# A two-layer hybrid block on one core: three layer norms summed by GpSimd, three residual groups turned by DMA

## Chip, cores, metric

One core of one Trainium2 chip. The metric is the device time of one execution in microseconds (us). The engines are TensorE (PE; its weight load is PEld), VectorE (DVE), ScalarE (ACT), GpSimd (POOL) and SyncE (SP), which here only issues DMAs.

## The reference

A sequence of 16 meta tokens and 256 input tokens (the padding ahead of them is masked), 1024 features, goes through two layers. Each has a mixer (retention, a gated recurrence and differential attention, gated and summed) and a convolutional feed-forward, each ahead of it a norm over features and behind it a residual sum; a last norm closes it:

```python
def _rms(x):
    xf = x.astype(F32)
    return xf * lax.rsqrt(jnp.mean(xf * xf, axis=-1, keepdims=True) + EPS)
...
    for li in range(DEPTH):
...
        h = h + mixer(rms_norm(h, norm_mix_g[li]), w_in[li], w_branch[li], w_out[li], lbs[li],
                      da_lambda[li], da_subln_g[li], lambda_init, valid, pos)
        h = h + conv_ffn(rms_norm(h, norm_ffn_g[li]), w_ffn_in[li], ffn_conv_w[li], ffn_conv_b[li],
                         w_ffn_out[li], valid)
    h = rms_norm(h, norm_final_g)
    return h[:, PAD:]
```

All arithmetic is float32.

## The kernel before

The residual stream `h` stays in SBUF with features on partitions: 8 blocks of 128 features by 272 tokens. All weights pass through one stream of 128x128 tiles in the order of their use, 8 tiles (512 KB) to a chunk. For each chunk SP loads `wraw` (3 buffers), ScalarE writes its rounded upper half `whi` (4 buffers) and VectorE the rest `wlo = wraw - whi` (4 buffers). A product of the stream is three TensorE matmuls, `whi` x upper half, `whi` x lower half, `wlo` x upper half of the moving operand (lines 940 to 942). One pair of output tiles takes 16 products where there are 1024 input features; the results lie in PSUM (`main`, 2 buffers of 2 banks; for some feed-forward pairs `fi`, from the pools `bank` and `acc` of 2 banks each). Helpers record all other operations, so most rows carry line 628.

**Order.** `_trace` runs over `ORDER`, the list of output pairs of a layer (projections, `b0` to `b2`, the output projection `wo`, the feed-forward input `fi` with 22 pairs, its output `fo`), and records each operation with a due time; `_Plan.order` then lays them out by a list scheduler with costs of its own, which decides the order on each engine. Every engine works its list strictly in that order. The stream's products keep their order on TensorE; other matmuls are placed between them.

**The norms.** `Norm.square` sums the squares of the 8 blocks to two sums per token and partition; `Norm.mean` adds these two and multiplies by `ones_d`, a 128x128 matrix of 1/1024, on TensorE (tile `ms`, a PSUM bank), which sums over partitions and repeats the mean on all of them. `Norm.finish` makes `rstd` of it, by a logarithm and an exponential on ScalarE. There are four: ahead of the mixer of layer one (at the kernel's start, with its adds on GpSimd), ahead of the feed-forward of layer one, ahead of the mixer of layer two and ahead of the feed-forward of layer two. In the third the last block comes late: `mean` runs on the other seven and `finish` adds a second matmul for the eighth (`self.rest`). Meanwhile the next stage's products already run on the unscaled `h`; the first four pairs are multiplied by `rstd` when they leave PSUM (`two_a`), and from the fifth pair on the input tiles `xh`, `xl` are made again from `y = h * rstd`.

**The last groups.** `final` computes the feed-forward output of layer two with tokens on partitions: four groups, 2 token blocks by 2 halves of 512 features, each in its own PSUM bank (`fo`), 22 products of three matmuls of 512 columns each (lines 1496 to 1498). The last three products of each group come group by group, so that the groups end 2.05 us after one another. The residual is brought to this layout by 16 TensorE transposes of `h` (4 per group), which are the first to write the banks; the products add to them. Then, per group, ScalarE squares (`sq`, with a sum per token), VectorE multiplies by the gain (`y`), and with both halves of a token block done their factor (`dm`) is applied and the rows are written to `out`.

Of the kernel before, what the change touches and what calls it, by code (L numbers as in the profile page):

```python
# [15 lines left out]
U16 = mybir.dt.uint16  # L16
AF = mybir.ActivationFunctionType
# [670 lines left out]
def _trace(ctx, tc, plan, a, depth, probe):  # L688
# [32 lines left out]
    def gate_tile(name):  # L721
        return new(gp, [P, KD, T], F32, "gate", 3, name)
# [7 lines left out]
    def bank(name):  # L730
        return new(bp, [P, 512], F32, "bank", 2, name)
# [108 lines left out]
    class Norm:  # L840
# [29 lines left out]
        def mean(self):  # L870

            tt(self.acc[:, 0, :], self.acc[:, 0, :], self.acc[:, 1, :], ADD)
            self.ps = bank("ms")[:, self.first : T]
            pe.matmul(self.ps, ones_d, self.acc[:, 0, :], start=True, stop=self.rest is None)

        def finish(self):
            if self.rest is None:
                self.mean()
            else:
                pe.matmul(self.ps, ones_d, self.rest, start=False, stop=True)  # L880
            rsqrt(rstd[:, self.first :], self.ps)

        def next(self):

# [134 lines left out]
    for li in range(depth):  # L1019
# [436 lines left out]
        def values(ps, vt, e):  # L1456
# [4 lines left out]
            to_tokens(src, vt, e)  # L1461
            return src

        def final():

            turns.pop(0)
            le_set()
            hi, lo = st["ghi"], st["glo"]
            accs = [[acc_bank("fo") for _ in range(2)], [bank("fo") for _ in range(2)]]
            plan.key = clock[0] - 6.0  # L1470
            gain = gate_tile("gain").rearrange("p k t -> p (k t)")[:, :D]
            sync.dma_start(gain, a["gl"])
            y = gate_tile("y").rearrange("p k t -> p (k t)")[:, : 2 * D].rearrange("p (t d) -> p t d", t=2)
            sq = gate_tile("sq").rearrange("p k t -> p (k t)")[:, : 2 * D].rearrange("p (t d) -> p t d", t=2)
            tokens = lambda t: slice(META + t * P, META + (t + 1) * P)
            plan.key = clock[0] - 1.0
            for t in range(2):
                for k in range(KD):
                    pe.matmul(accs[t][k // 4][:, k % 4 * P : (k % 4 + 1) * P], h[:, k, tokens(t)], ident, is_transpose=True, start=k % 4 == 0, stop=False)
            cost = 3 * (BANK / 2400 + 0.0133)  # L1480
            groups = [(t, c) for t in range(2) for c in range(2)]
            chunks = {}
            order = [(k, t, c) for k in range(FK - LATE) for t, c in groups]
            order += [(k, t, c) for t, c in groups for k in range(FK - LATE, FK)]
            red = temp(12, "dm")
            for k, t, c in order:
                plan.key = clock[0]
                if k not in chunks:
                    chunks[k] = weights.chunk()
                cols = slice(c * BANK, (c + 1) * BANK)  # L1490
                wh, wl = (x[:, cols] for x in chunks[k])
                gh, gl = (x[k // 4][:, k % 4, t * P : (t + 1) * P] for x in (hi, lo))
                o = accs[t][c]

                def run(o=o, wh=wh, wl=wl, gh=gh, gl=gl, end=k == FK - 1):
                    nc.tensor.matmul(o, gh, wh, start=False, stop=False)  # L1496
                    nc.tensor.matmul(o, gl, wh, start=False, stop=False)  # L1497
                    nc.tensor.matmul(o, gh, wl, start=False, stop=end)  # L1498

                plan.main.append(plan.add("pe", run, cost, [o], [wh, wl, gh, gl]))  # L1500
                clock[0] += cost
                if k < FK - 1:
                    continue
                plan.key = clock[0]
                ms = [red[:, 4 * t + i : 4 * t + i + 1] for i in range(4)]
                act.activation(sq[:, t, cols], o, AF.Square, accum_out=ms[c])
                if c == 0:

                    ts(ms[2], ms[0], 1.0 / D, EPS, MUL, ADD)
                    tt(y[:, t, cols], o, gain[:, cols], MUL)  # L1510
                    continue
                act.activation(ms[3], ms[1], AF.Ln, scale=1.0 / D, bias=ms[2])
                act.activation(ms[3], ms[3], AF.Exp, scale=-0.5)
                stt(y[:, t, cols], o, ms[3], gain[:, cols], MUL, MUL)
                act.activation(y[:, t, :BANK], y[:, t, :BANK], AF.Copy, scale=ms[3])
                for c, queue in ((1, sync), (0, act_queue)):
                    cols = slice(c * BANK, (c + 1) * BANK)
                    queue.dma_start(a["out"][:, t * D + c * BANK : t * D + (c + 1) * BANK], y[:, t, cols])

        for name, j in ORDER:  # L1520
# [112 lines left out]
            elif name == "fi":  # L1633
                ps = products(lambda k: x_tile(k, norm.folded), name, j, t0)
                first = META if last else 0
                if j % 4 == 0:
                    for n in ("ghi", "glo"):
                        g = slot(n, F32R)[:, : 4 * (T - first)]
                        st.setdefault(n, []).append(g.rearrange("p (a t) -> p a t", a=4))
                if j < ASIDE:  # L1640
                    plan.key += LATER
                u = ps if isinstance(ps, list) else [ps[:, f, :] for f in range(2)]
# [61 lines left out]
```

## Time and profile before

| | |
|---|---|
| runs | median 1282.17 us of 3 (1281.99 to 1282.75) |
| the profiled execution | 1282.95 us, span 1281.1 us |
| instructions in the span | 28467 |
| granted TensorE clock, mean | 0.997 |

The span runs from the first to the last instruction or transfer that the profile shows; the rest of the execution's time lies around it. Rows of a timeline give start, duration, engine, line, operation, output <- inputs and, in brackets, the engine's idle time before and what ended it. Rows of a tile give the least, median and largest duration in ns. In a list of waits stand the sum of us, the number of times and the longest.

### The profile page before, as it was taken

The numbers are of one execution on the slowest core, as the hardware profiler recorded it, in microseconds if no ns is written. First come the engines' busy times: TensorE is split into PE (matmuls) and PEld (weight loads), VectorE is DVE, ScalarE is ACT, GpSimd is POOL, SyncE is SP. The second block draws the span as 40 slices with busy tenths as digits, with TensorE's granted clock in tenths as the row PEclk, the third lists the DMA queues.
The fourth block names the chain that finished last, engine by engine and source line by source line (L and its number), as shares of the span: only waits on it lengthen the run. The fifth ranks groups of instructions, "written<-read, shape, count | busy, mean of one in ns | idle before, by whom it ended". The sixth has DMA issues, their size and how long they took to land.

```text
span 1281.1 us, 28467 instructions
## 1 busy us (share of the span) xinstructions
PE 1270.9 (99%) x11630; PEld 1248.0 (97%) x11630; DVE 934.8 (73%) x1601; ACT 858.9 (67%) x1498; POOL 101.1 (8%) x82
## 2 busy tenths in 40 slices
PE   9999999999999999999999999999999999999998
PEld 9999999999999999999999999999999999999986
DVE  6787476898575789886576774757976867898843
ACT  6766677759697576665456566776587975776643
POOL 3000041101111000000000000411011110000000
PEclk9999999999999999999999999999999999999999
DMA  7554557555746545556555545575556465465653
GB/s 266 196 167 155 161 163 196 170 181 149 206 125 213 182 153 194 179 169 195 172 175 181 166 152 180 162 202 166 182 155 215 150 204 196 154 211 183 212 186 111
DMA packets 100179, 228.50 MB, mean 178 GB/s; under 512 B 46288, under 2 KB 46416, under 8 KB 100048
## 3 DMA queue, kind: packets, MB, share of 16 engines
q1 hardware_dynamic: 99760, 226.15, 55.9%
q8 instruction: 91, 1.49, 0.5%
q10 hardware_dynamic: 288, 0.52, 0.1%
q14 instruction: 40, 0.33, 0.1%
HBM read 216.16 MB, written 1.05 MB: 170 GB/s over the span
## 4 chain that ended last, share of the span: by engine, by line
PE 98%; DMA 0%; DVE 0%; issue 0%; ACT 0%; SPq 0%
PE main L940 28%; PE main L941 28%; PE main L942 28%; PE fo L1496 2%; PE fo L1497 2%; PE fo L1498 2%; PE lev L1111 1%; PE fi L940 1%; PE fi L941 1%; PE fi L942 1%; PE ds L1359 1%; PE ho L628 1%; PE ro L628 1%; PE do L628 1%; PE s L628 0%; DMA wraw<-in_w 0%
## 5 line engine op out<-in xcount | busy, mean ns | idle before, releaser
L628 DVE TENSOR_TENSOR wlo<-wraw,whi 128x1024 fp32r<-128x1024 f32 (+1 forms) x411 | 501.9, 1225 | 224.4 <-ACT whi L628 222.7
L940 PE MATMUL main<-xh,whi 128*128 128x272 f32 (+1 forms) x2240 | 644.4, 288 | 2.6 <-ACT whi L628 1.3
L942 PE MATMUL main<-xh,wlo 128*128 128x272 f32 (+1 forms) x2240 | 636.8, 284 | 0.2 <-DVE wlo L628 0.2
L941 PE MATMUL main<-xl,whi 128*128 128x272 f32 (+1 forms) x2240 | 636.8, 284 | 0.0
L628 ACT ACTIVATE whi<-wraw 128x1024 fp32r<-128x1024 f32 (+1 forms) x411 | 426.5, 1041 | 209.4 <-PE main L941 123.3
L940 PEld LDWEIGHTS main<-xh,whi 128*128 128x128 f32 x2240 | 422.4, 189 | 3.2 <-ACT whi L628 1.5
L941 PEld LDWEIGHTS main<-xl,whi 128*128 128x128 f32 x2240 | 422.4, 189 | 1.3 <-issue 1.1
L942 PEld LDWEIGHTS main<-xh,wlo 128*128 128x128 f32 x2240 | 422.4, 189 | 0.4 <-DVE wlo L628 0.4
L628 POOL PARTITION_ALL_REDUCE hr<-hsq x36 | 71.9, 2023 | 564.2 <-ACT hsq L628 393.7
L628 DVE SCALAR_TENSOR_TENSOR two_b<-main,small,two_b 128x256 f32<-128x256 f32 (+2 forms) x128 | 54.4, 485 | 28.3 <-ACT two_b L628 28.3
L628 ACT ACTIVATE two_b<-main,small 128x272 f32<-128x272 f32 (+1 forms) x64 | 33.1, 568 | 31.1 <-PE main L942 30.4
L940 PE MATMUL main<-ghi,whi 128*128 128x272 f32 x176 | 51.0, 290 | 0.0
L941 PE MATMUL main<-glo,whi 128*128 128x272 f32 x176 | 50.6, 287 | 0.0
L942 PE MATMUL main<-ghi,wlo 128*128 128x272 f32 x176 | 50.3, 286 | 0.0
L940 PE MATMUL main<-b0hi,whi 128*128 128x272 f32 (+1 forms) x128 | 37.3, 291 | 0.0
L940 PE MATMUL main<-b1hi,whi 128*128 128x272 f32 (+1 forms) x128 | 37.1, 290 | 0.0
L940 PE MATMUL fi<-xh,whi 128*128 128x272 f32 (+1 forms) x128 | 36.6, 286 | 0.0
L940 PE MATMUL main<-yhi,whi 128*128 128x272 f32 (+1 forms) x128 | 36.4, 284 | 0.0
L942 PE MATMUL main<-yhi,wlo 128*128 128x272 f32 (+1 forms) x128 | 36.3, 284 | 0.0
L941 PE MATMUL main<-b1lo,whi 128*128 128x272 f32 (+1 forms) x128 | 36.3, 284 | 0.0
L941 PE MATMUL main<-ylo,whi 128*128 128x272 f32 (+1 forms) x128 | 36.3, 284 | 0.0
L941 PE MATMUL main<-b0lo,whi 128*128 128x272 f32 (+1 forms) x128 | 36.3, 284 | 0.0
(242 smaller groups left out, 2035.1 us busy)
## 6 DMA issues: line engine op xcount, KB each, us to landing
wraw<-in_w SPq DMA_DIRECT2D x402, 512.0 KB, 3.6
turned<-apart SPq DMA_TRANSPOSE x80, 2.5
h<-in_h SPq DMA_DIRECT2D x4, 272.0 KB, 6.3
dec<-in_dec SPq DMA_DIRECT2D x2, 544.0 KB, 4.5
wraw<-in_w SPq DMA_DIRECT2D x4, 256.0 KB, 5.2
const<-in_const SPq DMA_DIRECT2D x1, 937.0 KB, 8.0
gain<-in_gl SPq DMA_DIRECT2D x1, 512.0 KB, 4.7
out<-y ACTq DMA_DIRECT2D x2, 256.0 KB, 2.8
```

The lines of the kernel that those rows point to most:

```text
L628: self.plan.add(self.name, lambda: f(*args, **kw), cost, outs, ins, kind)
L940: nc.tensor.matmul(o, wh, hi, start=first, stop=False)
L941: nc.tensor.matmul(o, wh, lo, start=False, stop=False)
L942: nc.tensor.matmul(o, wl, hi, start=False, stop=last)
L1111: nc.tensor.matmul(o, keys, x, start=True, stop=True)
L1359: nc.tensor.matmul(ss[m][:, at : at + nk], q[half, hd, q0 : q0 + P], k[half, hd, :nk], start=True, stop=True)
L1496: nc.tensor.matmul(o, gh, wh, start=False, stop=False)
L1497: nc.tensor.matmul(o, gl, wh, start=False, stop=False)
L1498: nc.tensor.matmul(o, gh, wl, start=False, stop=end)
```

## The change

Two parts. First, the three norms whose adds are on VectorE no longer use TensorE: the two sums (and for the third norm the eighth block) are added by VectorE, GpSimd sums over the partitions (`partition_all_reduce`, as it does for the head norms already), and the logarithm takes 1/1024 as its scale. The norm at the start keeps its matmul. Second, of the four last groups only the last keeps its transposes. For the other three a new function `residual`, called at the third feed-forward pair of layer two, parts `h` into upper and lower 16-bit halves (`apart`), has SP turn each by a transposing DMA (`turned`), and joins them in `old`, with due times 20 us apart; the end of each such group adds `old` to the product on VectorE before the square.

```diff
         def mean(self):
             tt(self.acc[:, 0, :], self.acc[:, 0, :], self.acc[:, 1, :], ADD)
-            self.ps = bank("ms")[:, self.first : T]
-            pe.matmul(self.ps, ones_d, self.acc[:, 0, :], start=True, stop=self.rest is None)
+            if self.adds is pool:
+                self.ps = bank("ms")[:, self.first : T]
+                pe.matmul(self.ps, ones_d, self.acc[:, 0, :], start=True, stop=True)
 
         def finish(self):
             if self.rest is None:
                 self.mean()
             else:
-                pe.matmul(self.ps, ones_d, self.rest, start=False, stop=True)
-            rsqrt(rstd[:, self.first :], self.ps)
+                tt(self.acc[:, 0, :], self.acc[:, 0, :], self.rest, ADD)
+            if self.adds is pool:
+                rsqrt(rstd[:, self.first :], self.ps)
+                return
+            total = self.acc[:, 1, :]
+            pool.partition_all_reduce(total, self.acc[:, 0, :], P, ReduceOp.add)
+            rsqrt(rstd[:, self.first :], total, 1.0 / D)
...
+        def residual():
+
+            t = gate_tile("old").rearrange("p k t -> p (k t)")
+            st["sq"] = t[:, :BANK]
+            st["old"] = t[:, BANK : 4 * BANK].rearrange("p (g d) -> p g d", g=3)
+            plan.key = clock[0] + 20.0
+            for g, (t, c) in enumerate(((0, 0), (0, 1), (1, 0))):
+                apart, turned = planes("apart", 4 * P), planes("turned", 4 * P)
...
+                for i in range(2):
+                    act.activation(apart[:, i].rearrange("p (k x) -> p k x", k=4), halves(h[:, 4 * c : 4 * c + 4, META + t * P : META + (t + 1) * P], i), AF.Copy)
+                for i in range(2):
+                    sync.dma_start(turned[:, i].rearrange("p (b x) -> p b x", x=P), apart[:, i], transpose=True)
+                for i in range(2):
+                    act.activation(halves(st["old"][:, g : g + 1], i), turned[:, i].unsqueeze(1), AF.Copy)
+                plan.key += 20.0
...
-            for t in range(2):
-                for k in range(KD):
-                    pe.matmul(accs[t][k // 4][:, k % 4 * P : (k % 4 + 1) * P], h[:, k, tokens(t)], ident, is_transpose=True, start=k % 4 == 0, stop=False)
+            for k in range(4):
+                pe.matmul(accs[1][1][:, k * P : (k + 1) * P], h[:, 4 + k, tokens], ident, is_transpose=True, start=k == 0, stop=False)
...
-                act.activation(sq[:, t, cols], o, AF.Square, accum_out=ms[c])
+                if not turned:
+                    tt(y[:, t, cols], o, old[:, 2 * t + c], ADD)
+                    o = y[:, t, cols]
+                act.activation(sq, o, AF.Square, accum_out=ms[c])
```

What it does to the order on the engines is shown at three places. On TensorE, at the start of the last groups (`fo` are the four PSUM banks, `const` holds the identity matrix, `ghi` and `glo` the feed-forward's inner activations), there stood before:

```order
L942 MATMUL main_965_2180<-xh1_14_89,wlo381_2186 128x258
L628 MATMUL fo_967_2188<-const_4_79,h_3_78 128x128
L628 MATMUL fo_968_2189<-const_4_79,h_3_78 128x128
L628 MATMUL fo_969_2190<-const_4_79,h_3_78 128x128
L628 MATMUL fo_970_2191<-const_4_79,h_3_78 128x128
```

and so on to the sixteenth transpose. Now there stand:

```order
L948 MATMUL main_969_2184<-xh1_14_89,wlo381_2190 128x258
L1520 MATMUL fo_971_2192<-whi382_2200,ghi_899_1994 128x512
L1521 MATMUL fo_971_2192<-whi382_2200,glo_900_1995 128x512
L1522 MATMUL fo_971_2192<-wlo382_2201,ghi_899_1994 128x512
L1520 MATMUL fo_972_2193<-whi382_2200,ghi_899_1994 128x512
L1521 MATMUL fo_972_2193<-whi382_2200,glo_900_1995 128x512
L1522 MATMUL fo_972_2193<-wlo382_2201,ghi_899_1994 128x512
L1520 MATMUL fo_973_2194<-whi382_2200,ghi_899_1994 128x512
L1521 MATMUL fo_973_2194<-whi382_2200,glo_900_1995 128x512
L1522 MATMUL fo_973_2194<-wlo382_2201,ghi_899_1994 128x512
L628 MATMUL fo_974_2195<-const_4_79,h_3_78 128x128 x4
L1520 MATMUL fo_974_2195<-whi382_2200,ghi_899_1994 128x512
```

Twelve transposes are gone, and the other four stand behind the first product of three groups.

On ScalarE, at the norm ahead of the feed-forward of layer two (the number behind `whi` is that of the weight chunk), there stood before:

```order
L628 ACTIVATE whi343_2016<-wraw343_2015 128x1024
L583 ACT_TABLE_LOAD
L628 ACTIVATE rstd_18_93<-ms_900_1989,eps_9_84 128x272
L628 ACTIVATE rstd_18_93<-rstd_18_93 128x272
L628 ACTIVATE whi344_2023<-wraw344_2022 128x1024
L628 ACTIVATE two_b_905_2000<-two_a_904_1999,small_1_76 128x256 x2
```

and now:

```order
L628 ACTIVATE whi343_2013<-wraw343_2012 128x1024
L583 ACT_TABLE_LOAD
L628 ACTIVATE rstd_18_93<-sum_891_1962,eps_9_84 128x272
L628 ACTIVATE whi344_2027<-wraw344_2026 128x1024
L628 ACTIVATE rstd_18_93<-rstd_18_93 128x272
L628 ACTIVATE whi345_2030<-wraw345_2029 128x1024
```

The logarithm reads GpSimd's sum (`sum`) in place of TensorE's (`ms`), and the split of chunk 344 has moved between logarithm and exponential.

On ScalarE, at the end (the four squares, the factors `dm`, the scaling of a first half `y`, the output DMAs), there stood before:

```order
L628 ACTIVATE sq_973_2194,dm_974_2195<-fo_968_2189 128x512
L628 ACTIVATE dm_974_2195<-dm_974_2195 128x1 x2
L628 ACTIVATE y_972_2193<-y_972_2193,dm_974_2195 128x512
L628 DMA out<-y_972_2193 128x512
L628 ACTIVATE sq_973_2194,dm_974_2195<-fo_969_2190 128x512
L628 ACTIVATE sq_973_2194,dm_974_2195<-fo_970_2191 128x512
```

and now:

```order
L628 ACTIVATE old_908_2015,dm_977_2198<-y_976_2197 128x512 x2
L628 ACTIVATE dm_977_2198<-dm_977_2198 128x1 x2
L628 ACTIVATE y_976_2197<-y_976_2197,dm_977_2198 128x512
L628 ACTIVATE old_908_2015,dm_977_2198<-y_976_2197 128x512
L628 DMA out<-y_976_2197 128x512
L628 ACTIVATE old_908_2015,dm_977_2198<-fo_974_2195 128x512
```

Three squares read `y`, that is, VectorE's sum, in place of PSUM, and the first output DMA on this queue has moved behind the third square.

More of the change, by code (lines that the diff above doesn't have):

```diff
@@ L1462, in values @@
             return src
+        def residual():
[5 more added lines that the diff above has]
+                apart, turned = planes("apart", 4 * P), planes("turned", 4 * P)
+                halves = lambda x, i: x.bitcast(U16).rearrange("p k (x two) -> p k x two", two=2)[:, :, :, i]
+                for i in range(2):
[5 more added lines that the diff above has]
+                plan.key += 20.0
         def final():
@@ L1473, in final @@
             y = gate_tile("y").rearrange("p k t -> p (k t)")[:, : 2 * D].rearrange("p (t d) -> p t d", t=2)
-            sq = gate_tile("sq").rearrange("p k t -> p (k t)")[:, : 2 * D].rearrange("p (t d) -> p t d", t=2)
-            tokens = lambda t: slice(META + t * P, META + (t + 1) * P)
+            sq, old = st["sq"], st["old"]
+            tokens = slice(META + P, T)
             plan.key = clock[0] - 1.0
-            for t in range(2):
-                for k in range(KD):
-                    pe.matmul(accs[t][k // 4][:, k % 4 * P : (k % 4 + 1) * P], h[:, k, tokens(t)], ident, is_transpose=True, start=k % 4 == 0, stop=False)
+            for k in range(4):
+                pe.matmul(accs[1][1][:, k * P : (k + 1) * P], h[:, 4 + k, tokens], ident, is_transpose=True, start=k == 0, stop=False)
             cost = 3 * (BANK / 2400 + 0.0133)
@@ L1493, in final, with run @@
                 o = accs[t][c]
-                def run(o=o, wh=wh, wl=wl, gh=gh, gl=gl, end=k == FK - 1):
-                    nc.tensor.matmul(o, gh, wh, start=False, stop=False)
+                turned = (t, c) == (1, 1)
+                def run(o=o, wh=wh, wl=wl, gh=gh, gl=gl, first=k == 0 and not turned, end=k == FK - 1):
+                    nc.tensor.matmul(o, gh, wh, start=first, stop=False)
                     nc.tensor.matmul(o, gl, wh, start=False, stop=False)
@@ L1639, in _trace @@
                         st.setdefault(n, []).append(g.rearrange("p (a t) -> p a t", a=4))
+                if last and j == 2:
+                    key = plan.key
+                    residual()
+                    plan.key = key
                 if j < ASIDE:
```

## Prediction

> **What bounds the kernel now.** The first view is the page: busy time by engine, then the chain that ended last, by engine.
>
> ```profile
> PE 1270.9 (99%) x11630; PEld 1248.0 (97%) x11630; DVE 934.8 (73%) x1601; ACT 858.9 (67%) x1498; POOL 101.1 (8%) x82
> ...
> PE 98%; DMA 0%; DVE 0%; issue 0%; ACT 0%; SPq 0%
> ```
>
> TensorE is busy for 99% of the span, and 98% of the chain is TensorE's own work, one matmul released by the one ahead of it. The list of waits, for PE alone, says whether anybody ever holds it up:
>
> ```profile
> PE main L940 <- ACT whi L628: 1.3, 1, 1.3
> PE main L940 <- issue: 1.2, 1, 1.2
> ```
>
> These are the two largest; the other four of the list have 1.0 us or less each, one time each. A handful of us out of 1281.1, then. So the time is the sum of TensorE's instructions plus a short start and tail: what leaves TensorE's stream shortens the run one for one, unless something it waits for becomes late. The chain in order of time prices the instructions that leave:
>
> ```profile
> 463.95 0.46 PE ms L628 x2
> ...
> 650.28 0.46 PE ms L628 x2
> ...
> 657.68 0.46 PE ms L628 x2
> ...
> 1095.43 0.46 PE ms L628 x2
> ...
> 1213.53 1.75 PE fo L628 x16
> 1215.28 0.23 PE fo L1496
> ```
>
> All five stand on the chain, with no gap at either side (1213.53 + 1.75 = 1215.28).
>
> **What is removed.** Four norm matmuls go (each shown as two records): one after the layer-one output projection (463.95), two at the end of layer one (650.28 and 657.68), one after the layer-two projection (1095.43). 4 x 0.46 = 1.84 us. The first norm at the kernel's start keeps its own. Of the 16 transposes, 12 go: 1.75 x 12/16 = 1.31 us. Together **3.15 us**. The groups that no longer begin on a transpose begin on their first product, which was there already; the four transposes left only move behind nine products.
>
> **The norms: what comes instead, and what hides it.** The sum over features now runs on GpSimd, and the reciprocal root waits for that. The same operation stands in the trace for the head norms:
>
> ```profile
> L628 POOL PARTITION_ALL_REDUCE hr<-hsq x36: 1411/1884/2927, 159.3 to 1035.4; - x36
> ```
>
> So 1.9 us, at most 2.9. The tightest of the three places is the norm ahead of the layer-two feed-forward, because VectorE has nothing left there:
>
> ```profile
> 1105.00:1115.00 10.00, 10.00 (x88) 10.00 (x87) 10.00 (x21) 7.63 (x14) 0.00 (x0) 1.00 0.50 155
> 1115.00:1125.00 10.00, 10.00 (x88) 10.00 (x87) 10.00 (x19) 7.43 (x12) 0.00 (x0) 1.00 0.64 211
> 1125.00:1135.00 10.00, 10.00 (x88) 10.00 (x88) 10.00 (x20) 7.91 (x14) 0.00 (x0) 1.00 0.61 203
> ```
>
> After the stretch stand PE, weight load, VectorE, ScalarE, GpSimd: VectorE is full for 30 us, ScalarE at 7.4 to 7.9 of 10. Around the norm, the VectorE sum, ScalarE, and VectorE again:
>
> ```profile
> 1093.56 0.44 DVE L628 TENSOR_TENSOR sum<-sum 128x272 f32<-128x272 f32 x1
> ...
> 1096.43 1.28 ACT L583 ACT_TABLE_LOAD   x1
> 1097.72 0.49 ACT L628 ACTIVATE rstd<-ms,eps 128x272 f32<-128x272 f32 x1
> 1098.24 0.43 ACT L628 ACTIVATE rstd<-rstd 128x272 f32<-128x272 f32 x1
> 1098.64 1.07 ACT L628 ACTIVATE whi<-wraw 128x1024 fp32r<-128x1024 f32 x1
> ...
> 1098.71 0.70 DVE L628 TENSOR_TENSOR two_a<-main,rstd 128x516 f32<-128x516 f32 x1 [1.04 <-ACT rstd L628]
> ...
> 1113.50 1.32 DVE L628 SCALAR_TENSOR_TENSOR xl<-y,small,xh 128x272 fp32r<-128x272 f32 x3
> 1114.74 0.69 DVE L628 TENSOR_TENSOR two_a<-main,rstd 128x516 f32<-128x516 f32 x1
> 1115.35 1.22 DVE L628 TENSOR_TENSOR wlo<-wraw,whi 128x1024 fp32r<-128x1024 f32 x1
> ```
>
> The sum is complete at 1094.0. The all-reduce ends at 1095.9 (1096.9 at 2.9 us), and ScalarE cannot take the logarithm before 1097.72, since its table load stands ahead. The all-reduce is **covered** by 0.8 to 1.8 us. What does change is ScalarE's order: the next weight split (whi344) now stands between logarithm and exponential. It takes 1.07 us (the row at 1098.64 is the same work), so rstd comes about 1.0 us later, near 1099.6, and VectorE starts this backlog with the low half of that chunk at about 1099.3, not with the evacuation at 1098.71. The backlog holds the same instructions up to the row at 1115.35; it ends 0.6 us later, plus about 0.3 us of short waits for ScalarE on the way: 0.9 us. TensorE meanwhile arrives 0.46 us earlier.
>
> How much room is there? The stage's first product starts at 1089.66; a product is three matmuls, a pair of output tiles 16 products:
>
> ```profile
> 1089.66 0.28 PE L940 MATMUL main<-xh,whi 128*128 128x258 f32 x1
> 1089.78 0.28 PE L941 MATMUL main<-xl,whi 128*128 128x258 f32 x1
> ```
>
> At 0.117 us each, the fifth pair, the first to read the rescaled input, begins 64 x 3 x 0.117 + 0.46 (the norm matmul) later, at 1112.6, and wants input block 5 at 1116.2. That block is the first of the three in the row at 1113.50, done about 1114.0: 2.2 us of room. The weight chunk split at 1115.35 is the first of the sixth pair, wanted at 1112.6 + 5.6 + 0.2 = 1118.4 and done at 1116.6: 1.8 us. Each loses 0.9 + 0.46, so **0.4 to 0.8 us of room are left**. Cost: nothing, but the cover is thin, and each us beyond it is a us of the run. At the other two norms, VectorE and ScalarE have idle time at the place, and I count nothing.
>
> Does VectorE slow down beside an all-reduce? An earlier stage has the two side by side; the third and fourth rows are the place of the new all-reduce:
>
> ```profile
> 159.30 4.49 POOL L628 PARTITION_ALL_REDUCE hr<-hsq  x2 [129.70 <-ACT hsq L628]
> ...
> 162.09 2.06 DVE L628 TENSOR_TENSOR wlo<-wraw,whi 128x1024 fp32r<-128x1024 f32 x1 [1.96 <-ACT whi L628]
> ...
> 1093.92 1.22 DVE L628 TENSOR_TENSOR wlo<-wraw,whi 128x1024 fp32r<-128x1024 f32 x1
> 1096.44 1.23 DVE L628 TENSOR_TENSOR wlo<-wraw,whi 128x1024 fp32r<-128x1024 f32 x1 [1.30 <-ACT whi L628]
> ```
>
> It does: the split took 2.06 us instead of 1.22. At the new place the split beside it (1093.92) is followed by 1.30 us in which VectorE waits, so 0.8 us more are absorbed. The Trainium skill, "SBUF — State Buffer", section "Who interferes with whom", goes further: a VectorE operation with two SBUF inputs and a GpSimd one that reads SBUF exclude each other, the second waiting for the whole of the first. By that rule the all-reduce would begin only at 1095.1 and end at 1097.0 to 1098.0, so rstd could slip by up to 0.3 us more: the sum stays 3.05 us, but rival 1 gains. The rows show a slowing rather than a full block: the second all-reduce ended at 163.8, and a blocked split would have ended at 165.0, where this one ended at 164.15.
>
> **The residual: what comes instead.** Per group ScalarE copies two halves apart and two back, and SP issues two transposing DMAs:
>
> ```profile
> wraw<-in_w SPq DMA_DIRECT2D x402, 512.0 KB, 3.6
> ...
> L628 SPq DMA_TRANSPOSE turned<-apart x80: 1179/1247/2469, 120.6 to 1026.0; - x80
> ...
> L628 ACT ACTIVATE apart<-vsrc x48: 602/618/632, 119.9 to 959.8; 128x512 uint16<-128x512 uint16 x48
> ...
> L628 ACT ACTIVATE vt<-turned x32: 764/786/815, 123.7 to 964.6; 128x512 uint16<-128x512 uint16 x32
> ```
>
> The last three rows (ns: least, median, most) have the same size as the new ones, or about it; the first gives a weight load 3.6 us to land. ScalarE gains 2 x 0.62 + 2 x 0.79 = 2.8 us per group, 8.4 us in all, spread over some 60 us of the feed-forward where it has 2 to 3 us free in 10; cost nothing, bound 8.4 us if none of it fits. SP gains 6 x 1.25 = 7.5 us of issuing. In its queue the first transpose stands ahead of the load of chunk 351, which anyway waits for a buffer that the split of chunk 348 frees near 1117.5; the transpose's input, which ScalarE copies right behind its split of chunk 348, is ready near 1114, so it holds up nothing. Should it come late, the load behind it waits, and TensorE does once chunk 351 has used up its room: 1117.5 + 3.6 + 1.07 + 1.22 = 1123.4 against 1112.1 + 2.5 x 5.6 = 1126.1, at which the seventh pair's second half wants it, 2.7 us. The Trainium skill, "VectorE: DVE Perf Modes", sections "The three transpose paths" and "Rules for kernel authors", speaks against the move: a 128x128 transpose is quicker on TensorE (390 ns) than by DMA (1309 ns), and TensorE is to be used if PSUM may be the destination. By its figure twelve would be worth an estimated 4.7 us of TensorE time, and the sum would be 6.4 us; the chain has 0.11 us each and 1.31 us in all, and that stands. No wait for a turned block is in sight: the first is needed only at the very end, 100 us later.
>
> **The tail.** ScalarE and VectorE after the last products:
>
> ```profile
> 1269.80 0.69 DVE L628 TENSOR_TENSOR y<-fo,gain 128x512 f32<-128x512 f32 x1 [3.39 <-ACT sq L628]
> ...
> 1273.16 0.41 ACTq L628 DMA_DIRECT2D out<-y  x1
> 1273.88 0.60 ACT L628 ACTIVATE sq<-fo 128x512 f32<-128x512 f32 x1 [0.75 <-DVE y L628]
> ...
> 1275.19 0.60 ACT L628 ACTIVATE sq<-fo 128x512 f32<-128x512 f32 x1 [0.62 <-PE fo L1498]
> ```
>
> Each of three groups gets an add from PSUM (0.69, the nearest row) ahead of its square. For the third, the add can start at 1273.15 and end at 1273.84; its square runs to 1274.75 (0.6, and 0.2 for the accumulator, behind the scaling of the first half); then ScalarE issues an output DMA (0.41), which used to stand ahead of this square, and is free for the last square at about 1275.2, just when TensorE delivers it. I take 0.1 us; bounds 0 and 0.8 us (first outputs that land late beside the last ones). The last group's own chain is unchanged.
>
> **Sum.** 1.84 + 1.31 - 0.1 = 3.05 us. The profiled execution took 1282.95 us (span 1281.1), so its like would take 1279.9; from the median of the runs, 1282.17, it is **1279.1 us**, or 0.24% less.
>
> **Rivals.**
> 1. *The backlog eats part of it.* At the layer-two feed-forward the 0.4 to 0.8 us of room do not suffice: a stretch of 1 us by an all-reduce, or the two copies of the first group (1.2 us) ahead of a weight split, comes on top. For it: VectorE is at 10.00 of 10. Against: the new copies stand behind the split that is needed next. Loses 0.6 to 2 us: 1279.7 to 1281.1.
> 2. *The tail gives some back.* Up to 0.8 us: 1279.9.
> 3. *Slower: ScalarE has no time for the copies.* Place: the 60 us after 1112. If weight splits queue behind copies that wait for DMAs, VectorE's low halves follow late and TensorE waits for each. All 8.4 us on the path would give 1279.1 + 8.4 = 1287.5; it is slower by over 0.2% once 5.6 of the 8.4 us are on the path, that is, once ScalarE finds room for less than 0.9 of the 2.8 us in each 20. The rows give it 4.2 to 5.1 us free in 20, which speaks against it.
> 4. *It does not do what it says.* If the norm matmuls' time were waiting that moves on to the product behind, only the transposes would count: 1282.17 - 1.31 + 0.1 = 1281.0. Against: on the chain each begins where the matmul ahead of it ends.
>
> **How the numbers follow.** Forecast 0.64, rival 1 0.18, rival 2 0.08, rival 3 0.05, rival 4 0.05. About 0.2% (2.6 us) is what a measurement of this kernel can tell from no change; the line is 1279.6. The forecast lies 0.5 us inside it, so nearly all of its 0.64 counts as faster, and rivals 1, 2 and 4 as the same: faster 0.62, same 0.33, slower 0.05. The range goes from 1278.4 (all 3.15 us and 0.6 us of scatter, about the runs' own) to 1280.8, which leaves out rivals 3 and 4 and the end of rival 1.
>
> **What would show it.** Right: 16 instructions fewer in TensorE's list, the `ms` rows gone but for the first norm, four `fo` transposes, no longer list of TensorE's waits, and the last `fo` matmul ending about 3.1 us earlier against the span's start. Wrong: a wait of PE for `wlo` or `xl` between 1112 and 1140 (rival 1), for `whi` later (rival 3), or more than 5.9 us from the last matmul to the end (rival 2).

## The result and the profile after

The changed kernel takes 1278.97 us (median of 13 runs, 1277.74 to 1280.17) against 1281.23 us for the kernel before, run beside it (13 runs, 1280.30 to 1282.81): ratio 0.998, 95% interval 0.9972 to 0.9988. That is 2.3 us less, with an interval of 1.5 to 3.6. In a later series the two stood at 1278.75 and 1281.15 us. The forecast was 1279.1 us and 3.05 us less, from the 1282.17 us of the first three runs; those three lay 0.9 us above what the longer series gave. So the forecast time was met, while the difference came out 0.65 to 0.8 us smaller than forecast. The interval alone would still allow the 3.05 us; the trace, however, shows a wait that the forecast had put at nothing.

The page of the changed kernel, busy time and then the chain that ended last:

```profile
PE 1268.4 (99%) x11610; PEld 1245.0 (97%) x11610; DVE 935.3 (73%) x1605; ACT 863.4 (68%) x1510; POOL 108.3 (8%) x85
...
PE 95%; DVE 2%; DMA 1%; ACT 1%; issue 1%; SPq 0%; ACTq 0%; DVEq 0%
```

TensorE's share of the chain has dropped from 98% to 95%, and VectorE and DMA have come onto it. TensorE's list holds 20 records less than before, as announced: 16 instructions, and each norm matmul is shown as two records. The list of waits, for PE alone (sum of us, number of times, longest):

```profile
PE warm L628 <- POOL eps L628: 1.0, 1, 1.0
PE fi L948 <- DVE wlo L628: 0.9, 1, 0.9
PE main L948 <- issue: 0.4, 1, 0.4
PE main L948 <- DVE wlo L628: 0.4, 2, 0.2
```

The second row is new: a wait for a low half of a weight chunk (`wlo`), in the feed-forward of layer two. The chain in order of time (pieces under 0.1 us left out) shows what was behind it:

```profile
1108.70 0.13 PE fi L947
1108.84 0.90 DVE xl L628 x2
1109.74 1.14 DVE wlo L628
1110.88 0.68 DVE xl L628 x2
1111.62 0.49 DVE xl L628
1112.11 0.60 DVE two_a L628
1112.72 1.14 DVE wlo L628
1113.88 5.87 DMA wraw<-in_w
1119.83 1.07 ACT whi L628
1120.92 1.23 DVE wlo L628
...
1125.56 0.32 DVE wlo L628
```

Read it from the top. The chain leaves TensorE at 1108.84 and runs along VectorE's backlog behind the norm. The split at 1112.72 frees the buffer for the load of chunk 351; the load takes 5.87 us; then come ScalarE's and VectorE's halves of that chunk, work in VectorE's queue, and at 1125.56 the low half of chunk 352, for which TensorE waits:

```profile
1112.64 2.34 DVE L628 TENSOR_TENSOR wlo<-wraw,whi 128x1024 fp32r<-128x1024 f32 x2
...
1120.92 1.23 DVE L628 TENSOR_TENSOR wlo<-wraw,whi 128x1024 fp32r<-128x1024 f32 x1 [2.22 <-ACT whi L628]
...
1125.56 1.22 DVE L628 TENSOR_TENSOR wlo<-wraw,whi 128x1024 fp32r<-128x1024 f32 x1
1125.69 0.28 PE L947 MATMUL fi<-xl,whi 128*128 128x258 f32 x1
1126.83 0.39 PE L948 MATMUL fi<-xh,wlo 128*128 128x258 f32 x1 [0.86 <-DVE wlo L628]
1127.05 0.28 PE L946 MATMUL fi<-xh,whi 128*128 128x258 f32 x1
```

In a timeline the brackets hold the idle time ahead of an instruction. VectorE, which never idled from 1098.7 to past 1126 before, now stands idle for 2.22 us in the middle of its backlog, waiting for a load. TensorE's next two matmuls come 1.14 and 0.22 us after one another where 0.117 is its pace: 1.13 us lost. At 1143.67 the same happens once more, smaller, 0.49 us. Stage by stage, from the first record of each to the first of the next:

| | before | after | difference |
|---|---|---|---|
| span | 1281.1 | 1277.9 | -3.2 |
| start to the first `ms` matmul | 22.44 | 21.39 | -1.05 |
| the four norm matmuls | 1.84 | 0 | -1.84 |
| feed-forward input of layer two, without the norm matmul | 123.25 | 124.89 | +1.64 |
| last groups, first `fo` to the start of the last | 61.40 | 60.11 | -1.29 |
| start of the last `fo` matmul to the end | 6.33 | 6.53 | +0.20 |
| the rest | | | -0.86 |

The second row and the last are nothing that the change touches: the first weight load, and a wait for "issue" of 1.2 us in one list of waits and of 0.4 us in the other. They make up 1.9 of the 3.2 us between these two executions, so the two spans alone would flatter the change.

### The profile page after: what moved, and what is told of

Read it like the earlier page. It is cut to its first block, busy times and chain, and to the rows that moved or that the text cites. A ratio compares the mean times of both kernels' runs of the same rounds, so it can differ in the third digit from the quotient of the medians.

```text
span 1277.9 us, 28455 instructions
## 1 busy us (share of the span) xinstructions
PE 1268.4 (99%) x11610; PEld 1245.0 (97%) x11610; DVE 935.3 (73%) x1605; ACT 863.4 (68%) x1510; POOL 108.3 (8%) x85
## 3 DMA queue, kind: packets, MB, share of 16 engines
HBM read 216.16 MB, written 1.05 MB: 170 GB/s over the span
## 4 chain that ended last, share of the span: by engine, by line
PE 95%; DVE 2%; DMA 1%; ACT 1%; issue 1%; SPq 0%; ACTq 0%; DVEq 0%
PE main L946 27%; PE main L948 27%; PE main L947 27%; PE fo L1520 2%; PE fo L1521 2%; PE fo L1522 2%; PE lev L1117 1%; DMA wraw<-in_w 1%; PE ds L1365 1%; PE ho L628 1%; PE ro L628 1%; PE fi L947 1%; PE fi L946 1%; PE do L628 1%; PE fi L948 1%; DVE wlo L628 1%
## 5 line engine op out<-in xcount | busy, mean ns | idle before, releaser
L948 PE MATMUL fi<-xh,wlo 128*128 128x272 f32 (+1 forms) x128 | 36.3, 284 | 0.9 <-DVE wlo L628 0.9
```

Source lines behind the costliest of these rows:

```text
L948: nc.tensor.matmul(o, wl, hi, start=False, stop=last)
```

## Experiments

In the experiments' rows the code's lines are shifted by a few. "The stage" below is the layer-two feed-forward input, from its first product to the first matmul of the last groups; undisturbed it takes 123.2 us.

**The norms alone.** The residual as before (16 transposes), only the norms on GpSimd.

```diff
...
-                if last and j == 2:
-                    key = plan.key
-                    residual()
-                    plan.key = key
```

> The norms are summed on GpSimd as in the changed kernel; the residual is transposed on TensorE as before. The stage looked at is the layer-two feed-forward, from its first product to the first matmul of the last groups: 123.71 us before (with the norm matmul of 0.46), 124.89 us in the changed kernel, that is 1.64 us more than 123.25. Theory A (weight loads beside the transposing DMAs land late and VectorE's backlog turns that into a wait of TensorE): 123.25 us, no wait of TensorE there, and the run 1.8 us shorter than before. Rival B (the later reciprocal root alone uses up the room): 0.5 us or more of TensorE's wait for wlo or xl stays, 123.8 us or more. The three stretches with the four norm matmuls shorten by 1.84 us under both.

Measured: 1279.33 us, ratio 0.9986 (0.9977 to 0.9995), 1.84 us less. The stage took 123.57 us: 0.35 us of wait, at the same low half of chunk 352. The row of the chunk ahead of it on VectorE, chunk 351, shows the engine idle while the load of that chunk was under way:

```profile
1120.16 1.23 DVE L628 TENSOR_TENSOR wlo<-wraw,whi 128x1024 fp32r<-128x1024 f32 x1 [0.76 <-ACT whi L628]
```

So the norms alone already use up the room there, and a little more. The wait lies between the two expectations, none and 0.5 us or more: the transposing DMAs are not needed for it, and the late norm alone does not make 1.64 us.

**The residual alone.** The norms with their matmuls, the residual turned by DMA.

```diff
...
-            total = self.acc[:, 1, :]
-            pool.partition_all_reduce(total, self.acc[:, 0, :], P, ReduceOp.add)
-            rsqrt(rstd[:, self.first :], total, 1.0 / D)
+                pe.matmul(self.ps, ones_d, self.rest, start=False, stop=True)
+            rsqrt(rstd[:, self.first :], self.ps)
```

> The residual goes by DMA as in the changed kernel; the norms stay on TensorE. The same stage, 123.71 us before. Theory A with the room as forecast: VectorE's backlog starts 0.9 us earlier and TensorE comes 0.46 us later, so 1.4 us of the 1.6 us of wait are absorbed: 123.7 to 124.0 us. Theory A without any help of the room: 125.3 us. Rival B (the norm alone): 123.7 us. The transposes give 1.3 us, so the run is 0.9 to 1.3 us shorter than before (0.3 us longer if nothing is absorbed).

Measured: 1280.42 us, ratio 0.9997 (0.9988 to 1.0006), 0.75 us less; the interval is too wide to tell this from 0 or from 1.3. The trace is sharper: the last groups took 60.12 us (1.28 less) and the stage 123.70 with its norm matmul, 123.24 without, that is, no wait. Both expectations lay near 123.7 us, so this run does not part them; it does show that neither part alone makes the wait of 1.64 us. The load of chunk 351 took 4.4 us here.

**The residual 30 us later.** Copies and transposing DMAs come when VectorE's backlog is over.

```diff
-            plan.key = clock[0] + 20.0
+            plan.key = clock[0] + 50.0
```

> The changed kernel, with the three residual groups due 30 us later, when VectorE's backlog after the norm is gone. Theory A: loads beside transposes still take up to 6 us to land, but no wait of TensorE follows: the stage takes 123.25 us, and the run is 1.6 us shorter than the changed kernel, 3.0 to 3.2 us shorter than before. Rival B: the wait stays, 124 us or more. Theory C (ScalarE has no time for the copies): a wait moves to the new places, 124 us or more.

> The kernel with the residual's work 30 us later, a second profile. Theory: loads of chunks 351 and 352 land in at most 4.5 us, TensorE waits 0.5 us or less in the stage. Whether its pitch of 0.118 us behind 1126 belongs to the kernel: then the stage takes 124.0 us or more again; if it was this one execution, 123.3 to 123.7 us.

Measured: 1277.81 us, ratio 0.998 (0.9971 to 0.9989), 3.36 us less; the second profile's execution took 1277.64. TensorE's wait in the stage was 0.19 us in the first profile and none in the second. The first had a stage of 124.19 us all the same, because from 1126 on its matmuls came every 0.1178 us instead of 0.1166, at a granted clock of 1.00 in its rows; in the second they came every 0.1166 and the stage took 123.21. That pace belonged to one execution, and its cause is open.

**The exponential first.** The changed kernel, with ScalarE's split of chunk 344 queued behind the norm's exponential, as it stood before the change; the transposes stay where they are.

```diff
                     self.act.activation(to_hi, src, AF.Copy)
+                    if c == 344:
+                        self.plan.queue(self.plan.ops[-1], self.plan.exp)
...
             rsqrt(rstd[:, self.first :], total, 1.0 / D)
+            plan.exp = plan.ops[-1]
```

> The changed kernel, with the split of chunk 344 queued behind the exponential, so that the reciprocal root comes as early as before. Theory A with the room as forecast: VectorE's backlog is 0.9 us earlier, the wait of 1.64 us falls to 0.3 to 0.8 us, and the stage takes 123.6 to 124.0 us. If the order of these two does not matter: 124.9 us. The scheduler lays out the next 40 us somewhat differently, too, so 0.3 us either way tell nothing.

> The changed kernel with the split of chunk 344 queued behind the exponential, as in the run before. Theory (the order of logarithm, split and exponential is what takes VectorE's room): no wait in the layer-two feed-forward, stage 123.2 to 123.4 us, median 1277.8, about 1.0 to 1.4 us less than the changed kernel's. Rival (the stage's wait comes and goes by chance of the loads): a wait of 0.5 us or more shows again and the median is 1278.5 to 1279.

> The kernel with the exponential first, timed beside the changed kernel on one chip. Theory: no wait in the stage (123.2 us), median 0.8 to 1.6 us below the changed kernel's. Rival (the two orders are worth the same and the earlier difference was scatter between calls): medians within 0.4 us.

The norm's place in its timeline:

```profile
1094.17 0.52 ACT L628 ACTIVATE rstd<-sum,eps 128x272 f32<-128x272 f32 x1
1094.72 0.43 ACT L628 ACTIVATE rstd<-rstd 128x272 f32<-128x272 f32 x1
1095.06 1.05 ACT L628 ACTIVATE whi<-wraw 128x1024 fp32r<-128x1024 f32 x1
...
1095.19 0.70 DVE L628 TENSOR_TENSOR two_a<-main,rstd 128x516 f32<-128x516 f32 x1 [1.07 <-ACT rstd L628]
```

The exponential follows the logarithm, and VectorE takes the first evacuation (`two_a`) 9.1 us after the stage's first product at 1086.10, against 10.8 us in the changed kernel. Measured three times: 1277.82 us (ratio 0.9972, 0.9962 to 0.9981), 1278.06 (0.9974, 0.9965 to 0.9984) and 1277.87 (0.9974, 0.9965 to 0.9984). The stage took 123.21, 123.21 and 123.20 us, with no wait. Timed beside the changed kernel (1278.75 us) it is 0.88 us lower. That is more than expected: 0.3 to 0.8 us of wait were to be left. The reason lies in the loads as well as in the norm. The load of chunk 351 was issued 27.05 us after the stage's first product, 0.45 us sooner than in the changed kernel, and took 4.4 to 4.9 us where it takes 5.5 and 5.9 there. Chunk 352 is done 1.2 to 2.0 us sooner, of which only 0.45 us is the sooner issue and the rest the shorter load. So the wait goes when the norm comes early, and the transposes then cost TensorE nothing; that it goes through VectorE's earlier start alone is not shown. This is the best version of the study, level with the one whose residual comes later.

**The changed kernel again**, a second profile.

> The changed kernel itself, unedited, a second profile of it. If the wait of 1.64 us in the layer-two feed-forward is the kernel's own: chunks 351 and 352 land in 5.5 to 6 us again, TensorE loses 1.3 to 1.9 us in the stage (124.5 to 125.2 us), and the median is about 1279.0. If the size of it is chance of the loads: the two land in 4.4 to 5 us as in the kernels with the copies left out or the exponential first, and TensorE loses 0.3 to 0.9 us (stage 123.5 to 124.2).

Its SP queue, and VectorE at the same place:

```profile
1115.07 1.46 SPq L628 DMA_DIRECT2D wraw<-in_w  x2
1116.58 1.39 SPq L628 DMA_TRANSPOSE turned<-apart  x1
...
1121.77 1.23 DVE L628 TENSOR_TENSOR wlo<-wraw,whi 128x1024 fp32r<-128x1024 f32 x1 [1.88 <-ACT whi L628]
```

Measured: 1278.75 us, ratio 0.9983 (0.9974 to 0.9992); stage 124.48 us, a wait of 1.23 us. The two loads landed in 5.5 and 5.7 us and VectorE stood idle for 1.88 us. The wait is the kernel's own, a little smaller here.

**Without the transposing DMAs; without ScalarE's copies; without the copies back alone.** Three variants on why the loads are slow, each with the planned order of the changed kernel and one execution. Each edit is shown by its main line; the expectation behind it says the rest.

```diff
-                    sync.dma_start(turned[:, i].rearrange("p (b x) -> p b x", x=P), apart[:, i], transpose=True)
+                    plan.add("sp", lambda: None, 0.06 + 4 / 360e3 * 4 * P * P + 0.7, [turned[:, i]], [apart[:, i]])
...
```

> Left out: the six transposing DMAs; ScalarE's copies back read the parted halves instead, so three groups of the residual are not turned. All else, and the planned order of every engine, is as in the changed kernel. Theory (the transposes stretch the two weight loads beside them, chunks 351 and 352): these two loads land in 3.2 to 4.2 us in place of 5.9 and 6.0, and the layer-two feed-forward stage (first product to first matmul of the last groups) takes 123.25 to 123.7 us in place of 124.89. Rival (the two loads are slow because they are issued back to back, when two low halves of weights are done back to back): they still land in 5 to 6 us and the stage takes 124.5 us or more. The last groups' stage stays at 60.11 us in both.

```diff
-                    act.activation(apart[:, i].rearrange("p (k x) -> p k x", k=4), halves(h[:, 4 * c : 4 * c + 4, META + t * P : META + (t + 1) * P], i), AF.Copy)
+                    plan.add("act", lambda: None, 0.105 + 0.833e-3 * 4 * P, [apart[:, i]], [src], AF.Copy)
...
```

> Left out: ScalarE's twelve copies; the transposing DMAs read raw halves of the residual stream without waiting for anybody, and the residual of three groups is missing from the output (zeros are added). The planned order is as in the changed kernel. If ScalarE's copies, standing ahead of weight splits, are what uses up VectorE's room, the stage loses its wait (123.25 to 123.6 us); if it is the loads beside the transposes, the stage keeps 0.8 us or more of wait (124.0 or more) as long as a transpose and the loads of chunks 351 and 352 still meet.

```diff
-                    act.activation(halves(st["old"][:, g : g + 1], i), turned[:, i].unsqueeze(1), AF.Copy)
+                    out = halves(st["old"][:, g : g + 1], i)
+                    run = (lambda: nc.gpsimd.memset(st["old"], 0.0)) if g == 0 and i == 0 else (lambda: None)
+                    plan.add("act", run, 0.105 + 0.833e-3 * 4 * P + 0.33e-3 * 4 * P, [out], [turned[:, i]], AF.Copy)
```

> Left out: ScalarE's six copies back only (zeros stand in their place in the output's residual of three groups); the six copies that part the halves and the six transposing DMAs stay, in the planned order of the changed kernel. The changed kernel's loads of chunks 351 and 352 took 5.5 to 6.0 us in two profiles, 4.6 and 4.7 with all twelve copies left out. If the parted halves or the transposes' start have to do with it, the loads take 5.4 us or more again and TensorE loses 0.8 us or more in the stage; if the copies back have, which run while the loads are under way, they take 4.4 to 5.0 us and the stage loses 0.3 us or less.

The list of DMA issues, narrowed to the load of chunk 351 and then to that of chunk 352 (last number: us from issue to landing), first of the changed kernel:

```profile
wraw<-in_w SPq DMA_DIRECT2D x1, 512.0 KB, 5.9
...
wraw<-in_w SPq DMA_DIRECT2D x1, 512.0 KB, 6.0
```

then without the transposing DMAs:

```profile
wraw<-in_w SPq DMA_DIRECT2D x1, 512.0 KB, 4.4
...
wraw<-in_w SPq DMA_DIRECT2D x1, 512.0 KB, 4.5
```

and without the copies back:

```profile
wraw<-in_w SPq DMA_DIRECT2D x1, 512.0 KB, 4.3
...
wraw<-in_w SPq DMA_DIRECT2D x1, 512.0 KB, 4.6
```

Each of the three brings them to 4.3 to 4.7 us (4.6 and 4.7 without the copies). All profiles side by side; "done" is the end of chunk 352's low half on VectorE, counted from the stage's first product, and TensorE wants it at 39.44 us (39.90 before and with the residual alone, with the norm matmul), so the room is the difference:

| kernel | load of 351 | done | room | TensorE's wait in the stage |
|---|---|---|---|---|
| before | 3.7 | 38.19 | 1.71 | 0 |
| norms alone | 4.7 | 39.63 | -0.19 | 0.35 |
| residual alone | 4.4 | 38.39 | 1.51 | 0 |
| changed | 5.9 | 40.41 | -0.97 | 1.64 |
| changed, again | 5.5 | 40.07 | -0.63 | 1.23 |
| 30 us later, two profiles | 4.6, 4.2 | 39.47, 39.11 | -0.03, 0.33 | 0.19, 0 |
| no transposing DMAs | 4.4 | 38.90 | 0.54 | 0.39 (at 1143) |
| no copies | 4.6 | 39.11 | 0.33 | 0 |
| no copies back | 4.3 | 38.84 | 0.60 | 0 |
| exponential first, three profiles | 4.9, 4.5, 4.4 | 38.91, 38.49, 38.41 | 0.53, 0.95, 1.03 | 0 |
| the same, all four groups turned (below) | 4.6 | 38.63 | 0.81 | 0 |

Two of my readings fall here. That two loads issued back to back are enough to make them slow is not it: in all three variants they are issued 1.1 us apart, as in the changed kernel, and take 4.3 to 4.7 us. That the transposing DMAs alone stretch the load to 5.9 is not it either: with the copies left out, or the exponential first, they lie beside the same loads and these take 4.3 to 4.9. What the runs show is that the load of chunk 351 takes 4.2 to 4.9 us in every kernel but two: 3.7 in the kernel before, and 5.5 and 5.9 in the changed one, where the late norm, the transposing DMAs and the copies back come together.

One more transfer stands in the traces at this place. DMAs also bring in instructions, and one such packet of 16 KB falls into the load of chunk 351; of the changed kernel's queues between 1116 and 1117 us (packets, MB, share of 16 engines):

```profile
q8 instruction: 1, 0.02, 12.5%
```

Over the changed kernel's whole trace, weight loads with nothing else beside them have a median of 3.3 us, with another weight load 3.9, with both that and such a packet 4.2, and with a transposing DMA as well 4.8 (four fifths of them between 3.6 and 5.6). The load of chunk 351 meets all three in the changed kernel, and also in the variants without the copies or the copies back and with the exponential first. In the changed kernel's two profiles the packet starts 2.6 and 3.3 us after the load's issue; with the copies or the copies back left out, or the exponential first, 1.0 to 1.2 us after it; with the norms alone 2.4 (load 4.7) and without the transposing DMAs 2.2 (load 4.4). No run moves the packet by itself, so whether it delays the load or is held up with it stays open, and so does what makes 5.5 to 6.0 us out of 4.3 to 4.9.

**All four groups turned by DMA**, with the exponential first: no transpose is left on TensorE in the last groups.

```diff
-            for g, (t, c) in enumerate(((0, 0), (0, 1), (1, 0))):
+            for g, (t, c) in enumerate(((0, 0), (0, 1), (1, 0), (1, 1))):
...
-                turned = (t, c) == (1, 1)
+                turned = False
```

> As the kernel with the exponential first, and the last group turned by DMA too: no residual transpose on TensorE is left. If TensorE's time is all that counts: 4 x 0.11 = 0.44 us less (about 1277.4). Theory: the add of 0.69 us now stands between the last matmul and the last square, where nothing hides it, so the tail grows from 6.58 to about 7.3 us, the last groups' stage falls from 60.11 to 59.67, and the sum is 0.25 us slower than the kernel with the exponential first (about 1278.1).

Its end, from the last matmul's start:

```profile
1269.71 0.39 PE L1521 MATMUL fo<-wlo,ghi 128*128 128x512 f32 x1
1270.31 0.68 DVE L628 TENSOR_TENSOR y<-fo,old 128x512 f32<-128x512 f32 x1
1271.08 0.63 ACT L628 ACTIVATE gain<-y 128x512 f32<-128x512 f32 x1 [1.48 <-DVE y L628]
```

Measured: 1278.20 us, ratio 0.9979 (0.9969 to 0.9988), against 1278.06 for the exponential first, timed beside it. The last groups took 59.62 us (0.49 less), the end 7.3 us (0.8 more than its 6.5): 0.3 us worse by the trace, 0.14 by medians, too little to be told apart by these runs. The add of 0.68 us stands between the last matmul and the last square, where nothing hides it. By the trace the change does well to leave the last group's transposes on TensorE; the times do not settle it.

## Why the prediction came out as it did, point by point

- **What is removed: right.** Four norm matmuls and twelve transposes are gone. At the layer-one output projection the step from its last matmul to the second one of the next stage fell from 0.71 to 0.25 us, 0.46 as forecast; the last groups fell by 1.29 us (forecast 1.31). The last matmul does end 3.4 us earlier against the span's start, where about 3.1 was to be the sign; but 1.9 us of that is the scatter named above, so this sign was met by luck. The Trainium skill, "VectorE: DVE Perf Modes", section "The three transpose paths", gives the 390 ns named in the prediction for bf16; the twelve transposes here, float32 and one behind another, were worth 0.11 us of TensorE each.
- **The all-reduce is covered: right.** The place in the changed kernel:

```profile
1090.62 1.22 DVE L628 TENSOR_TENSOR wlo<-wraw,whi 128x1024 fp32r<-128x1024 f32 x1
1090.87 2.71 POOL L628 PARTITION_ALL_REDUCE sum<-sum  x1 [57.68 <-DVE sum L628]
...
1093.14 1.28 ACT L583 ACT_TABLE_LOAD   x1
...
1094.43 0.52 ACT L628 ACTIVATE rstd<-sum,eps 128x272 f32<-128x272 f32 x1
1094.90 1.06 ACT L628 ACTIVATE whi<-wraw 128x1024 fp32r<-128x1024 f32 x1
1095.87 0.41 ACT L628 ACTIVATE rstd<-rstd 128x272 f32<-128x272 f32 x1
1096.00 1.23 DVE L628 TENSOR_TENSOR wlo<-wraw,whi 128x1024 fp32r<-128x1024 f32 x1 [1.62 <-ACT whi L628]
1097.14 0.69 DVE L628 TENSOR_TENSOR two_a<-main,rstd 128x516 f32<-128x516 f32 x1
```

  It took 2.71 us, inside the bounds of 1.9 and 2.9, ended at 1093.58 and left 0.85 us until the logarithm at 1094.43. VectorE's split beside it took 1.22 us, so it was not slowed to 2.06 as in an earlier stage; here the split had begun first. It was the all-reduce that paid. Eight others of like size (128x272 or 128x258), none of which began during a VectorE operation with two SBUF inputs, show what it takes by itself (ns: least, median, most):

```profile
L628 POOL PARTITION_ALL_REDUCE hr<-sum x8: 1847/1865/1885, 233.6 to 894.5; - x8
```

  It took 0.85 us more than these, and the split still had 0.97 us to run when it began; at the layer-one output projection, where the split had as long to run, it took 2.71 us too. The rule that the prediction takes from the Trainium skill, "SBUF — State Buffer", section "Who interferes with whom", fits this: by it, at the median length of 1.9 us, the all-reduce was to end 7.3 us after the stage's first product, without it 6.2, and it ended at 7.2. GpSimd's rows are rough, so the fit is no proof. The prediction's "a slowing rather than a full block" was read off a split that began during an all-reduce, the other order. For TensorE nothing hung on it.
- **The late reciprocal root: right where it looked; the room failed further on.** ScalarE's split between logarithm and exponential made it about 1 us later, as worked out. At the sixth pair's first chunk (348) the room fell from 1.80 to 0.75 us with the norms alone, where 0.4 was forecast. The step that failed is "0.4 to 0.8 us of room are left", taken for the whole stage. The tight spot is four chunks further on, chunk 352, the first of the eighth pair: its room went from 1.71 us before to -0.19 with the norms alone, a loss of 1.90 us where 0.9 + 0.46 = 1.36 was counted. The term that was left out is VectorE's wait of 0.76 us for the load of chunk 351, which took 4.7 us. Without it, by estimate, 0.57 us of room would have been left.
- **"Of the transposes: holds up nothing": the second failed step.** I gave the load of chunk 351 3.6 us and 2.7 us of room. It took 5.9 and 5.5 us, so VectorE idled for 2.22 and 1.88 us in mid-backlog, and that time was missing at chunk 352. For chunk 351 itself the room did suffice: its low half was done 0.9 and 1.2 us before TensorE wanted it. What the step overlooked is that an engine that is full all the time cannot catch up on an idle stretch before its next due piece.
- **Rival 1 happened, beside the forecast's removals.** Its sign, a wait for `wlo` between 1112 and 1140, shows at 1126 (the smaller wait at 1144 lies just behind); its size, 0.6 to 2 us, fits 1.64 and 1.23 us. As differences, the measured 2.3 and 2.4 us less lie in its range (1.1 to 2.5 less) and short of the forecast. Its causes do not fit. There was no stretch of VectorE beside the all-reduce, and no copy stood ahead of the late split on ScalarE, which waited for the load. The late norm and slow loads did it together: in the runs that take away either, at most 0.39 us of wait remains.
- **The tail: 0.2 us in place of 0.1**, within 0 to 0.8. ScalarE was free for the last square, as forecast (it idled 0.59 us ahead of it). The end comes 4.01 us after the issue of the last output at 1273.89, where it was 3.87 before; the remaining 0.06 us lie ahead of the last square. The sign named for rival 2, more than 5.9 us from the last matmul to the end, does not part the two: from that matmul's end it was about 5.9 us before and 6.1 now.

```profile
1270.55 0.62 ACT L628 ACTIVATE old<-y 128x512 f32<-128x512 f32 x1
1270.68 0.38 ACTq L628 DMA_DIRECT2D out<-y  x1
...
1271.85 0.60 ACT L628 ACTIVATE old<-fo 128x512 f32<-128x512 f32 x1 [0.59 <-PE fo L1522]
...
1273.89 0.36 ACTq L628 DMA_DIRECT2D out<-y  x1
```

- **Rivals 3 and 4 did not happen.** ScalarE found time for its copies, and the norm matmuls' time was work, not waiting.
- **Why the time was met nonetheless.** Without the wait, the kernel with the exponential first is 3.35, 3.09 and 3.28 us below the kernel before: the forecast's 3.05 us is what the change brings when the room holds. The changed kernel gives 0.9 us of it back; that the forecast time fits all the same is owed to the three first runs, which lay 0.9 us high. Two errors of one size cancelled, which is luck.

## What to carry to other kernels

Where one engine is full for tens of us, ask for each piece due behind the edit how late it may come, and count in that sum the time that the engine would stand idle for a load, at the longest landing time of that stage and not at the median. Two edits that draw on the same room are best weighed as one: here the norms alone gave 0.35 us of wait, the residual alone none, both together 1.2 to 1.6 us. When an instruction gets a later input, look at what a list scheduler slips in ahead of it: here moving one weight split back behind the exponential gave 0.9 us by the medians and the best kernel, in part through a shorter load whose cause is open.

## What the runs showed of the hardware

- A 512 KB weight load took 3.1 to 3.5 us when little else was under way, 3.7 us at the place above in the kernel before, 4.2 to 4.9 us there in the other kernels, and 5.5 to 6.0 us in the changed kernel. The transposing DMAs of the residual took 1.2 to 1.9 us of SP's queue and landed in 2.5 to 6.2 us.
- All-reduces by GpSimd took 1.85 to 1.89 us where none of VectorE's two-input SBUF operations was under way at their start, and 2.71 us where such an operation had 0.97 us left to run.
- In one execution TensorE's pace in the stage changed from 0.1166 to 0.1178 us a matmul at a granted clock of 1.00; in the same kernel's second profile it did not.
